# Two thirds of a modulation vector: summed over weight rows on GpSimd instead of TensorE

## The chip, the cores and the metric

The kernel runs on one core of one Trainium2 chip, in one launch. The metric is the device time of an execution in microseconds. TensorE is PE in the profile (PEld is its weight load), VectorE is DVE, ScalarE is ACT, GpSimd is POOL, and SyncE, which only issues transfers here, is SP.

## What is computed

One transformer block on 1024 tokens of width 1024, in fp32. A vector `c` gives six modulation vectors of 1024 (shift, scale and gate, for the mixer and for the feed-forward part); the mixer is a dilated attention with 8 heads beside a gated DeltaNet with 8 heads.

```python
c_act = jax.nn.silu(c)                        # c: (1, 1024)
mod = c_act @ w_ada[l] + b_ada[l]             # w_ada: 1024 x 6144
sh1, sc1, g1, sh2, sc2, g2 = [m[:, None, :] for m in jnp.split(mod, 6, axis=-1)]
h = _rmsnorm(x, norm_attn_g[l]) * (1.0 + sc1) + sh1
proj = h @ w_in[l]
q_a, k_a, v_a, q_d, k_d, v_d, z_d, b_d, a_d = jnp.split(proj, split_points, axis=-1)
y_attn = _dilated_attention(q_a, k_a, v_a, rel_bias)
y_delta = _gated_deltanet(q_d, k_d, v_d, z_d, b_d, a_d, ...)   # conv, chunked delta rule, gate z
x = x + g1 * (jnp.concatenate([y_attn, y_delta], axis=-1) @ w_out[l])
h = _rmsnorm(x, norm_ffn_g[l]) * (1.0 + sc2) + sh2
x = x + g2 * ((jax.nn.silu(h @ w_gate[l]) * (h @ w_up[l])) @ w_down[l])
return _rmsnorm(x, final_norm_g)
```

The change concerns `mod`. Only `sh1` and `sc1`, the first third, are needed before the projections. `g1`, `sh2`, `sc2` and `g2`, the last two thirds, are needed only after attention and DeltaNet.

## The kernel before

**Stages.** The first 16 column tiles of `mod` (a tile is 128 columns) are made at the start. Then come the projections, the DeltaNet in two groups of four heads (`delta(0)`, `delta(1)`), the attention in four pairs of heads (`attend`), the output projection, and from about 820 us on a feed-forward part, in which POOL has no instruction.

**Projections.** A weight slab of 128 x 512 is loaded on SP's queue into one of 3 buffers, copied by ACT to a rounded high part, and POOL subtracts to get the low part (`wsplit`, L209; subtraction L216; 5 buffers each for the two parts). TensorE multiplies high by high, high by low and low by high (`gemm`, L567, and `proj_t`, L590). The slabs of the delta projections of group 1 are named kd, qd and vd, those of the gates z0 and z1, those of the attention va (values) and a (keys and queries).

**Order.** Most of these projections are filler. `others()` (L1103) is a generator that yields after every few matmuls: z0; kd, qd and vd of group 1; z1; va; then the keys and queries of the four attention pairs. The DeltaNet and the attention are written in the order of their dependencies, and at named places (`turn`, `hold`, `until`, with amounts in microseconds from a table, `FILL`, and `LEVELS`) they take the next pieces from the generator. So TensorE's order is fixed when the program is built, and a matmul that waits holds up all behind it.

**The delta rule's chain.** For each group, a decay table goes out to `G_d` and comes back as `dt` tiles, masked by POOL (L692). `delta_inverse` inverts 32 x 32 triangles in 31 steps, each a multiplication (L862, `tm`) and an addition (L866, `tt`) on DVE. The result goes through DRAM and comes back as `tn`. Then four heads follow, staggered by `SKEW`: TensorE's `lv` (L894), `lw` (L923), `lx` (L931); DVE's transposes of `tn` into `U` (L899) and products (L905, L925); POOL clears `U` (L895) and part of `tc` (L896) first. A scan over chunks (`delta_scan`) follows. In attention, POOL and ACT share the scaling of the exponentials `X` (POOL L1263, ACT L1261), and POOL makes `KL` (L1227).

**The modulation before.** `modulation()` (L1081) has 64 steps: 8 groups `i` of four column tiles, times 8 blocks `k` of 128 rows. A step loads a 128 x 512 slab `wm` of `w_ada` (L1091, 256 KB) and issues `rows4` (L196): four matmuls, the slab as moving operand, and as weights a window of 32 columns of `cc`, the activated `c` laid out by blocks. The sums of a group gather in one PSUM bank. After eight steps DVE transposes them (`mt`, L203) and adds `b_ada` (L207). `mixed()` (L1123) wraps `others()`: whenever 1.9 us (`MODS`) of filler have been issued, and no head of the delta rule is being written (`quiet`), it issues the next step. What is left goes out ahead of the attention (`run(mods)`, L1193). The slabs share their three buffers (tag `tc`) with the `tc` tiles of the heads.

Of the kernel before, what the change touches and what calls it, by code (L numbers as in the profile page):

```python
# [18 lines left out]
P = 128  # L19
# [8 lines left out]
TCB = 3  # L28
MODS = 1.9
EARLY = 1  # L30
# [39 lines left out]
def build(tc, I, out):  # L70
# [47 lines left out]


    pd, sd = pool("pd")  # L120
    wp, swp = pool("wp", side="right")
# [23 lines left out]
    def ybank(name):  # L145
        return psb(name, "y", 1)
# [62 lines left out]
    def wsplit(src, n, name, eng=None, hurry=True):  # L209
        raw = wp.tile([P, slot], F32, name=f"wr_{name}", tag="wr", bufs=3)  # L210
        hi = wp.tile([P, slot], F32R, name=f"wh_{name}", tag="wh", bufs=5)
        lo = wp.tile([P, slot], F32R, name=f"wl_{name}", tag="wl", bufs=5)
        with urgent() if hurry else ExitStack():
            nc.sync.dma_start(raw[:, :n], src)
            nc.scalar.copy(hi[:, :n], raw[:, :n])
            (eng or nc.gpsimd).tensor_tensor(  # L216
                out=lo[:, :n], in0=raw[:, :n], in1=hi[:, :n].bitcast(F32), op=ALU.subtract
            )
        return hi, lo


# [621 lines left out]
    def delta_inverse(g, st):  # L843
# [92 lines left out]
        for step in range(3 * SKEW + 8):  # L936
            if step % SKEW == 0 and step // SKEW < 4:
                heads.append(head(step // SKEW))
            with hold(*LEVELS[g]) if step == 0 else ExitStack():
                quiet[0] = True  # L940
                for h in heads:
                    next(h, None)
        quiet[0] = False

# [135 lines left out]

    def modulation():  # L1081
        pm = ybank("mods")
        for i in range(8):
            t0 = 16 + 4 * i
            ps = pm[:, P * (i % 4) : P * (i % 4 + 1)]
            if i % 4 == 0:
                nc.vector.memset(pm, 0.0)
            for k in range(KT):
                w = pd.tile([P, HALF], F32, name=f"wm_{i}_{k}", tag="tc", bufs=TCB)
                with urgent():  # L1090
                    nc.sync.dma_start(w, I["wada"][k * P : (k + 1) * P, t0 * P : t0 * P + HALF])  # L1091
                rows4(ps, cc[:, k : k + 32], w, 4, k == KT - 1)
                yield
            t = pv.tile([P, 256], F32, name=f"mt{i}", tag="zt", bufs=2)
            by_columns(ps, mod[:, t0 : t0 + 4], 4, bada[:, t0 : t0 + 4], shape=t)
        nc.vector.scalar_tensor_tensor(
            out=G2, in0=mod[:, 32:40], scalar=1.0, in1=gff, op0=ALU.add, op1=ALU.mult
        )

    done = set()  # L1100
    mods = modulation()
# [90 lines left out]
    until(lambda: EARLY - 1 in done)  # L1192
    run(mods)  # L1193

# [149 lines left out]
    attend(range(EARLY))  # L1344
    run(fill[0])
    sh_.close()
    py, sy = pool("py", side="right")
# [18 lines left out]
    for k in range(EARLY):  # L1366
        y_load(k, _.ya[k])
    run(fill[0])

    ps = abank("g2t")  # L1370
# [4 lines left out]

    sa.close()
    syd.close()
    pf, sf = pool("pf")
# [503 lines left out]
```

## Time and profile before

| | |
|---|---|
| time, median of 3 executions | 1454.71 us (1454.52 to 1459.43) |
| the profiled execution's own time | 1459.26 us |
| its span, first to last instruction | 1457.5 us |
| mean granted TensorE clock | 0.975 of full speed |
| PE busy | 1381.9 us, 95% of the span |
| DVE, ACT, POOL busy | 872.7, 668.8, 284.5 us |
| POOL instructions | 267 |
| modulation's matmul records (L196) | 512, from 117.2 to 399.8 us, 8 a step |
| modulation's loads | 64 of 256 KB, 3.6 us from issue to landing |

A row of the profile's timelines gives the start, the duration, the engine, the line, the operation, output <- inputs, and, in brackets, the idle time of the engine just before it and what ended it. `x8` at the end of a row means that eight instructions that touch are shown as one. A row of groups gives, after `|`, the busy time in us and the mean of one instruction in ns, then the idle time before them.

### The profile page before, as it was taken

How to read it: one execution, taken by the hardware profiler on the slowest of the kernel's cores; microseconds unless marked ns; L12 is line 12 of the kernel's file. 1: busy time of each engine (PE TensorE's matmuls, PEld its weight loads, DVE VectorE, ACT ScalarE, POOL GpSimd, SP SyncE). 2: the span in 40 equal slices, each digit the busy share in tenths (PEclk: the TensorE clock that was granted, in tenths of full speed). 3: DMA queues.
4: the chain of work that ended last, by engine and by line, in shares of the span. 5: the costliest groups of instructions: out<-in, count | busy, mean ns of one | idle time of the engine just before them, and what ended most of it. 6: DMA issues, size and time to landing. Idle time of an engine off the chain costs nothing.

```text
span 1457.5 us, 24558 instructions
## 1 busy us (share of the span) xinstructions
PE 1381.9 (95%) x8984; PEld 1121.6 (77%) x8984; DVE 872.7 (60%) x1676; ACT 668.8 (46%) x1279; POOL 284.5 (20%) x267
## 2 busy tenths in 40 slices
PE   7998989998999989999999889999999999999997
PEld 4777857787888768778877668888888888888886
DVE  3686762665746151466426985767666676565477
ACT  3487513348233363566337733333333333444446
POOL 1343412243323333344244000000000000000000
PEclk9998999998999989999999989999999999999999
DMA  8736464465531626643275443545454465866566
GB/s 306 251 106 175 134 192 142 146 197 168 157 107 56 179 78 181 169 121 95 92 226 168 136 151 117 192 137 175 148 167 156 155 207 182 277 211 202 198 218 238
DMA packets 171345, 244.64 MB, mean 168 GB/s; under 512 B 33014, under 2 KB 76327, under 8 KB 171224
## 3 DMA queue, kind: packets, MB, share of 16 engines
q1 hardware_dynamic: 171224, 243.07, 53.0%
q8 instruction: 71, 1.16, 0.3%
q14 instruction: 50, 0.41, 0.1%
HBM read 180.25 MB, written 67.48 MB: 170 GB/s over the span
## 4 chain that ended last, share of the span: by engine, by line
PE 63%; DVE 6%; DMA 4%; ACT 3%; issue 2%; POOL 1%; SPq 0%; ACTq 0%; DVEq 0%; POOLq 0%
PE wga L1513 8%; PE wua L1513 8%; PE X L1699 6%; PE g_a L567 5%; PE wuc L1513 4%; PE wgc L1513 4%; PE Z L1699 4%; PE wo L567 4%; PE g_va L590 3%; PE y L1293 3%; PE tr L1276 2%; PE Y L1699 2%; PE wub L1513 2%; PE wgb L1513 2%; PE S L1252 1%
## 5 line engine op out<-in xcount | busy, mean ns | idle before, releaser
L1503 DVE TENSOR_TENSOR wl_db<-wr_db,wh_db 128x512 fp32r<-128x512 f32 x77 | 53.2, 691 | 75.6 <-ACT wh_db L1502 75.5
L1502 ACT CAST wh_db<-wr_db 128x512 fp32r<-128x512 f32 x77 | 47.9, 622 | 97.8 <-PE X L1699 41.3
L1699 PE MATMUL X<-wl_db,wh_da 128*128 128x512 f32 x176 | 68.5, 389 | 0.0
L1699 PE MATMUL X<-wh_db,wl_da 128*128 128x512 f32 x176 | 68.5, 389 | 0.0
L1699 PE MATMUL X<-wh_db,wh_da 128*128 128x512 f32 x176 | 68.5, 389 | 0.0
L1263 POOL TENSOR_SCALAR X<-X,sc 128x128 f32<-128x128 f32 (+7 forms) x64 | 47.6, 747 | 70.6 <-DVE sc L1262 56.2
L1261 ACT ACTIVATE X<-X,sc 128x128 f32<-128x128 f32 (+7 forms) x64 | 49.6, 776 | 22.4 <-DVE sc L1256 17.2
L1256 DVE CUSTOM_DVE_ANT_0 X<-S,ng 128x512 f32<-128x512 f32 (+3 forms) x64 | 36.8, 586 | 35.0 <-PE S L1253 26.3
L567 PE MATMUL wo<-yh,wh_wo 128*128 128x512 f32 x128 | 52.2, 409 | 3.7 <-ACT yh L1359 2.1
L1503 DVE TENSOR_TENSOR wl_da<-wr_da,wh_da 128x512 fp32r<-128x512 f32 x77 | 52.7, 686 | 1.2 <-ACT wh_da L1502 1.2
L567 PE MATMUL g_a<-hh,wh_a 128*128 128x512 f32 x128 | 51.4, 401 | 0.0
L567 PE MATMUL g_a<-hl,wh_a 128*128 128x512 f32 x128 | 51.1, 399 | 0.0
L567 PE MATMUL g_a<-hh,wl_a 128*128 128x512 f32 x128 | 51.0, 398 | 0.0
L567 PE MATMUL wo<-yl,wh_wo 128*128 128x512 f32 x128 | 51.0, 398 | 0.0
L567 PE MATMUL wo<-yh,wl_wo 128*128 128x512 f32 x128 | 50.5, 396 | 0.0
L1502 ACT CAST wh_da<-wr_da 128x512 fp32r<-128x512 f32 x77 | 47.4, 616 | 5.9 <-PE wua L1513 5.8
L1222 DVE SCALAR_TENSOR_TENSOR QS<-raw,QS 64x1024 fp32r<-64x1024 f32 x8 | 12.6, 1571 | 61.4 <-ACT QS L1221 61.4
L1502 ACT CAST wh_wg_s<-wg_s 128x512 fp32r<-128x512 f32 x33 | 20.5, 622 | 58.1 <-PE wuc L1513 22.6
L1293 PE MATMUL y<-et,va 128*64 128x128 f32 x576 | 46.7, 289 | 0.0
L1276 PE MATMUL tr<-ident,X 128*128 128x128 f32 x288 | 45.0, 282 | 1.6 <-ACT et L1281 1.2
L1502 ACT CAST wh_wg<-wr_wg 128x512 fp32r<-128x512 f32 x33 | 20.4, 622 | 51.4 <-issue 20.0
L1293 PEld LDWEIGHTS y<-et,va 128*64 128x64 f32 x576 | 35.0, 142 | 10.4 <-issue 8.8
(530 smaller groups left out, 4391.4 us busy)
## 6 DMA issues: line engine op xcount, KB each, us to landing
wr_da<-ao_d SPq DMA_DIRECT2D x77, 256.0 KB, 3.1
wm<-in_wada SPq DMA_DIRECT2D x64, 256.0 KB, 3.6
wr_wg<-in_wg SPq DMA_DIRECT2D x48, 256.0 KB, 2.9
wr_wu<-in_wu SPq DMA_DIRECT2D x48, 256.0 KB, 2.7
ao_d<-a SPq DMA_DIRECT2D x44, 256.0 KB, 2.2
wr_wd<-in_wdn SPq DMA_DIRECT2D x44, 256.0 KB, 3.0
wr_db<-wt_d SPq DMA_DIRECT2D x44, 256.0 KB, 2.6
ao_d<-as SPq DMA_DIRECT2D x33, 256.0 KB, 2.0
```

Of the source, the lines that this page charges most:

```text
L567: last[0] = nc.tensor.matmul(ps, a[:, w0], b[k0 + k4][:, cs], start=(i == 0), stop=(i == n - 1))
L590: last[0] = nc.tensor.matmul(ps[:, :n], a[k][:, ts_], b[:, w0], start=(i == 0), stop=(i == 23))
L1252: nc.tensor.matmul(ps[:, 0 : c1 - c0], QS[:, qs], KS[:, c0:c1], start=True, stop=False)
L1256: nc.vector.tensor_tensor_reduce(out=X[:, c0:c1], in0=ps[:, 0 : c1 - c0], in1=ng[:, u + c0 : u + c1], scale=1.0, scalar=(3e38 if m is None ...
L1261: nc.scalar.activation(X[:, 0:nk], X[:, 0:nk], AF.Exp, scale=-1.0, bias=m, accum_out=sc[:, 2:3])
L1263: nc.gpsimd.tensor_scalar(out=X[:, 0:nk], in0=X[:, 0:nk], scalar1=sc[:, 3:4], scalar2=0.0, op0=ALU.mult, op1=ALU.add)
L1276: nc.tensor.transpose(ps[:, (kb - c0) * P : (kb - c0 + 1) * P], X[:, kb * P : kb * P + P], ident)
L1293: nc.tensor.matmul(yps[64 * e : 64 * e + 64, yc], va[:, kb, 64 * e : 64 * e + 64], ets[e][:, kb, :], start=(kb == 0), stop=(kb == qb),)
L1502: nc.scalar.copy(hi, src)
L1503: (eng or nc.vector).tensor_tensor(out=lo, in0=src, in1=hi.bitcast(F32), op=ALU.subtract)
L1513: nc.tensor.matmul(ps, a[:, w0], b, start=(first and k == 0 and n_ == 0), stop=(k == 3 and n_ == 2), skip_group_check=True,)
L1699: nc.tensor.matmul(bank[b], a[:, ts_], w, start=(first and f == 0 and n_ == 0), stop=(f == NF - 1 and n_ == 2), skip_group_check=True,)
```

## The change

The 64 steps leave TensorE. A step is now tied to a weight slab: `wsplit`, after issuing its own load and subtraction, calls `mod_steps(steps[0], ...)`, which issues, for each step, the load of the slab `wm` two steps ahead, on SP behind the weight slab's load, and two instructions on GpSimd behind the subtraction: `wm` times the block's column of `c` (a scalar per partition), and for `k` > 0 an addition into an accumulator `wa` (at `k` = 0 the product is written there directly). There is one step with each slab until the values of attention, two with each slab of the keys and queries, and one with each of the first slabs of the output projection. The slabs have a pool of their own, `pm`: three buffers `wm` and four `wa`. When a group of column tiles is finished, five steps later `mod_columns` sums its accumulator over the partitions: four matmuls with 128 x 128 of the accumulator as weights and a column of ones, and an addition of `b_ada` on DVE. The last group's sums come just before `g2` is needed.

```diff
@@ wsplit
-            nc.sync.dma_start(raw[:, :n], src)
+            ld = nc.sync.dma_start(raw[:, :n], src)
             nc.scalar.copy(hi[:, :n], raw[:, :n])
-            (eng or nc.gpsimd).tensor_tensor(
+            sp = (eng or nc.gpsimd).tensor_tensor(
                 out=lo[:, :n], in0=raw[:, :n], in1=hi[:, :n].bitcast(F32), op=ALU.subtract
             )
+        if steps[0]:
+            mod_steps(steps[0], ld, sp)
         return hi, lo
+
+    steps = [0]
@@ modulation() removed, in its place:
+    MU = [(t0, k) for t0 in range(16, 48, 4) for k in range(KT)]
+    wms2, accs = {}, {}
+    at = [0]
...
+    def mod_load2(u):
+        if u < len(MU):
+            t0, k = MU[u]
+            wms2[u] = pm.tile([P, HALF], F32, name=f"wm_{t0}_{k}", tag="wm", bufs=3)
+            nc.sync.dma_start(wms2[u], I["wada"][k * P : (k + 1) * P, t0 * P : t0 * P + HALF])
+
+    def mod_steps(n, ld, sp):
+        for _n in range(n):
+            u = at[0]
+            if u == len(MU):
+                return
+            at[0] += 1
+            t0, k = MU[u]
+            with tc.issue_after(ld.ins):
+                if u == 0:
+                    mod_load2(0)
+                    mod_load2(1)
+                mod_load2(u + 2)
+            w = wms2.pop(u)
+            if k == 0:
+                accs[t0] = pm.tile([P, HALF], F32, name=f"wa_{t0}", tag="wa", bufs=4)
+            o = accs[t0] if k == 0 else w
+            with tc.issue_after(sp.ins):
+                nc.gpsimd.tensor_scalar(
+                    out=o, in0=w, scalar1=cc[:, k : k + 1], scalar2=0.0, op0=ALU.mult, op1=ALU.add
+                )
+                if k > 0:
+                    nc.gpsimd.tensor_tensor(out=accs[t0], in0=accs[t0], in1=w, op=ALU.add)
+            if k == 5 and t0 > 16:
+                mod_columns(t0 - 4)
+
+    def mod_columns(t0):
+        with tc.issue_after(last[0].ins):
+            ps = abank(f"mods{t0}")
+            for j in range(4):
+                nc.tensor.matmul(ps[:, j : j + 1], accs[t0][:, j * P : (j + 1) * P], ones[:, 0:1], start=True, stop=True)
+        nc.vector.tensor_tensor(out=mod[:, t0 : t0 + 4], in0=ps[:, 0:4], in1=bada[:, t0 : t0 + 4], op=ALU.add)
...
@@ others()
+        steps[0] = 1
         yield from proj_t(I["wz0"], 256, "z0", z_evac(0))
...
         done.add("va")
+        steps[0] = 2
         for hp in range(4):
...
-    def mixed():
-        t = 0.0
-        for c in others():
-            yield c
-            t += c
-            if t > MODS and not quiet[0]:
-                t = 0.0
-                next(mods, None)
-    quiet = [False]
-    fill[0] = mixed()
+    fill[0] = others()
@@ 
-    run(mods)
@@ after the first attention pair
+    steps[0] = 1
@@ after the last filler of attention
+    mod_columns(44)
```

The amounts in `FILL` and `LEVELS` are the same. A pool is opened and closed for `pm`, and the buffer that the program sets aside for dynamic transfers is given a size of 256, which leaves SBUF for it.

More of the change, by code (lines that the diff above doesn't have):

```diff
@@ L28 @@
 TCB = 3
-MODS = 1.9
 EARLY = 1
@@ L117, in small @@
         return t
+    pm, sm = pool("pm")
     pd, sd = pool("pd")
@@ L939, in delta_inverse @@
             with hold(*LEVELS[g]) if step == 0 else ExitStack():
-                quiet[0] = True
                 for h in heads:
                     next(h, None)
-        quiet[0] = False
     def delta_scan(g, st):
@@ L1078, in va_end @@
         return g
[L1081 to L1098, printed above, removed]
+    MU = [(t0, k) for t0 in range(16, 48, 4) for k in range(KT)]
@@ new lines, in build @@
+    wms2, accs = {}, {}
+    at = [0]
+    pmods = [None]
+    def mod_load2(u):
[27 more added lines that the diff above has]
+                mod_columns(t0 - 4)
@@ new lines, in mod_columns @@
+    def mod_columns(t0):
[4 more added lines that the diff above has]
+        nc.vector.tensor_tensor(out=mod[:, t0 : t0 + 4], in0=ps[:, 0:4], in1=bada[:, t0 : t0 + 4], op=ALU.add)
+        if t0 == 36:
+            nc.vector.scalar_tensor_tensor(
+                out=G2, in0=mod[:, 32:40], scalar=1.0, in1=gff, op0=ALU.add, op1=ALU.mult
+            )
@@ L1100, in build @@
     done = set()
-    mods = modulation()
     def others():
@@ L1368, in build @@
     run(fill[0])
+    assert at[0] == len(MU)
+    mod_columns(44)
     ps = abank("g2t")
@@ L1376, in build @@
     sa.close()
+    sm.close()
+    steps[0] = 0
     syd.close()
@@ L1870 @@
     from concourse.bass_utils import run_bass_kernel_spmd as _run
-    nc = _bacc.Bacc("TRN2", target_bir_lowering=False, num_devices=1)
+    nc = _bacc.Bacc("TRN2", target_bir_lowering=False, num_devices=1, dynamic_dma_scratch_size=256)
     arrays, aps = {}, {}
```

## The prediction

> **What bounds the kernel now.** I began with the page's busy shares, then cut the stretch in which the modulation runs into slices of 40 us, and read the timelines of three engines where two of them meet.
>
> ```profile
> PE 1381.9 (95%) x8984; PEld 1121.6 (77%) x8984; DVE 872.7 (60%) x1676; ACT 668.8 (46%) x1279; POOL 284.5 (20%) x267
> ```
>
> TensorE is busy for 95% of the span and GpSimd for 20%, so a change that takes work from the first to the second looks free. Two of the slices (columns: window, its length, busy time and instructions of PE, weight load, DVE, ACT, POOL, then granted clock, DMA share and GB/s) show that this isn't one regime.
>
> ```profile
> 160.00:200.00 40.00, 35.65 (x244) 26.30 (x243) 35.83 (x74) 8.88 (x17) 13.65 (x13) 0.91 0.54 162
> 200.00:240.00 40.00, 39.96 (x258) 26.94 (x258) 8.21 (x13) 11.07 (x24) 8.59 (x9) 1.00 0.79 230
> ```
>
> At 200 to 240 PE is full and DVE nearly empty: matrix work binds. At 160 to 200 DVE is the full one, with the inverse of the delta rule's first group (L862 and L866, 31 dependent steps). Which of the two arrives later at the next step that needs both, the heads at L894, is shown by the timelines of PE and of DVE before the first head.
>
> ```profile
> 238.39 0.39 PE L567 MATMUL g_vd<-hl,wh_vd 128*128 128x512 f32 x1
> 238.61 0.39 PE L567 MATMUL g_vd<-hh,wl_vd 128*128 128x512 f32 x1
> 238.93 0.43 PE L196 MATMUL mods<-wm,cc 128*32 128x128 f32 x8
> 239.29 0.50 PE L567 MATMUL g_vd<-hh,wh_vd 128*128 128x512 f32 x1
> 239.62 0.39 PE L567 MATMUL g_vd<-hl,wh_vd 128*128 128x512 f32 x1
> 239.86 0.39 PE L567 MATMUL g_vd<-hh,wl_vd 128*128 128x512 f32 x1
> ...
> 240.88 1.20 PE L894 MATMUL lv<-tn,dt 32*32 32x32 f32 x64
> ```
> ```profile
> 211.93 0.88 DVE L899 STREAM_TRANSPOSE U<-tn 32x256 f32<-32x256 f32 x2
> ...
> 214.08 0.44 DVE L899 STREAM_TRANSPOSE U<-tn 32x256 f32<-32x256 f32 x1
> 234.07 0.32 DVE L203 STREAM_TRANSPOSE mt<-mods 128x128 f32<-128x128 f32 x1 [19.54 <-PE mods L196]
> ```
>
> The inverse's result is in SBUF by 211.93, for DVE transposes it there, and is ready at 214.5; PE comes to the head only at 240.88. So the chain has about 26 us of slack at the first group, and PE sets the time. At the second group it is otherwise:
>
> ```profile
> 405.31 0.19 DVE L866 TENSOR_TENSOR tt<-tt,tm 128x31 f32<-128x31 f32 x1
> 413.37 1.78 DVE L899 STREAM_TRANSPOSE U<-tn 32x256 f32<-32x256 f32 x4 [7.86 <-DMA tn<-tn_d]
> 420.76 1.75 DVE L905 TENSOR_TENSOR cs<-lv,nbp 32x256 f32<-32x256 f32 x4 [5.61 <-PE lv L894]
> ```
>
> The transposes end at 415.15 and the head's first result comes 5.61 us later. The slack is about 5 us: less PE work is hardly felt there, and a later DVE is.
>
> **Removed from PE.** A step's eight matmul records stand between 512-column matmuls. Those follow each other in 0.22 to 0.24 us; across the step it is 0.68 (238.61 to 239.29), then 0.33. One step therefore takes 0.45 + 0.10 = 0.55 us. The records of the modulation by window, in the same columns without ACT and POOL, are
>
> ```profile
> 120.00:160.00 40.00, 3.81 (x56) 1.29 (x56) 0.00 (x0) 0.83 0.59 152
> 160.00:200.00 40.00, 5.15 (x88) 1.82 (x88) 0.61 (x2) 0.91 0.54 162
> 200.00:240.00 40.00, 6.39 (x120) 2.36 (x120) 1.12 (x3) 1.00 0.79 230
> ```
>
> 264 records at 8 a step are 33 of the 64 steps, 18.2 us before the first head. Two stalls of the modulation go as well:
>
> ```profile
> 136.17 0.63 PE L196 MATMUL mods<-wm,cc 128*32 128x128 f32 x8 [3.18 <-DMA wm<-in_wada]
> 191.43 0.65 PE L196 MATMUL mods<-wm,cc 128*32 128x128 f32 x8 [3.89 <-DVE mt L203]
> ```
>
> 7.1 us, so PE alone could be 25 us earlier at the first head; with the 31 later steps (17 us) the whole kernel has some 42 us to win.
>
> **Added to GpSimd.** Each step is one 128x512 multiplication by a scalar and, for seven of eight, one 128x512 addition. Rows of those shapes on POOL:
>
> ```profile
> L1263 POOL TENSOR_SCALAR X<-X,sc 128x512 f32<-128x512 f32 x8 | 5.5, 693 | 12.9 <-DVE sc L1262 8.0 <-PE S L1253 4.1 <-PE tr L1276 0.8
> L216 POOL TENSOR_TENSOR wl_vd<-wr_vd,wh_vd 128x512 fp32r<-128x512 f32 x4 | 5.1, 1284 | 23.1 <-ACT wh_vd L215 23.1
> ```
>
> 64 x 0.693 + 56 x 1.284 = 116 us, 1.98 us for a full step. POOL goes to about 400 us, far from full, so its throughput isn't the matter. What matters is who waits while it is busy. The first cost is DVE: in the inverse, an instruction of this size passes in 0.41 us (183.78), except beside POOL's subtractions.
>
> ```profile
> 182.37 1.37 DVE L862 TENSOR_TENSOR tm<-nt,tt 128x240 f32<-128x240 f32 x1
> 183.78 0.41 DVE L866 TENSOR_TENSOR tt<-tt,tm 128x240 f32<-128x240 f32 x1
> ...
> 185.58 1.45 DVE L866 TENSOR_TENSOR tt<-tt,tm 128x252 f32<-128x252 f32 x1
> ```
> ```profile
> 169.12 4.69 POOL L216 TENSOR_TENSOR wl_kd<-wr_kd,wh_kd 128x512 fp32r<-128x512 f32 x3
> 173.76 0.74 POOL L612 TENSOR_TENSOR zt<-zt,ngh 128x256 f32<-128x256 f32 x1
> 174.58 1.29 POOL L216 TENSOR_TENSOR wl_qd<-wr_qd,wh_qd 128x512 fp32r<-128x512 f32 x1
> 182.10 1.38 POOL L216 TENSOR_TENSOR wl_qd<-wr_qd,wh_qd 128x512 fp32r<-128x512 f32 x1 [6.23 <-ACT wh_qd L215]
> 185.46 1.29 POOL L216 TENSOR_TENSOR wl_qd<-wr_qd,wh_qd 128x512 fp32r<-128x512 f32 x1 [1.99 <-ACT wh_qd L215]
> ```
>
> The DVE instruction at 182.37 lies under POOL's at 182.10, the one at 185.58 under 185.46; together they lose 2.0 us to 2.67 us of POOL, 0.75 us for each. I take 0.75 for all of a step. The Trainium skill ("SBUF — State Buffer", section "Who interferes with whom") says that a DVE instruction with two SBUF inputs and a GpSimd instruction that reads SBUF exclude each other for a whole instruction. By that rule a step would cost the chain up to 1.98 us rather than 1.5; the row has 0.75 of it, and the sum goes by the row.
>
> Six of the slabs' subtractions lie in this inverse, and each now has a step behind it; with one from a later slab I count seven. 7 x 1.98 x 0.75 = 10.4 us on the first inverse (7 if only the additions block, 14 if all does). Ahead of it, three of the modulation's loads now wait on the SP queue for GpSimd's additions to free their buffers, and in the changed order the decay table's store and load (G_d, dt) stand behind them there, which the chain needs before the inverse: at most three steps of 1.98 us, so 0 to 6; I take 3. The chain is ready for the head at 214.5 + 10 + 3 = 228 instead of 214.5. PE comes there at 240.9 - 25 = 216. So the chain takes over as the bound, and the first head is 13 us earlier, not 25. If its first matmul needs the inverse alone and not the transposes, the gain is 3 to 5 us larger: I take 15 (8 to 25).
>
> **From the first heads to the second inverse.** About half of the 31 later steps go from PE here (9 us), but the order in which the changed program issues puts 6 to 12 us more projection work ahead of this group's preparation. I take 0, from -5 to +9.
>
> **Second inverse and heads.** Five steps behind the wva slabs: 5 x 1.98 x 0.75 = 7.4 us; the slack of 5 takes up most, so 2.5 (0 to 8). Then the heads clear U on POOL, in the midst of their chain:
>
> ```profile
> 424.55 0.96 POOL L895 MEMSET U<- 128x1024 f32 x1 [20.79 <-PE lw L923]
> 426.92 0.30 POOL L896 MEMSET tc<- 32x256 f32 x1 [1.41 <-PE lx L931]
> 430.15 0.96 POOL L895 MEMSET U<- 128x1024 f32 x1 [2.93 <-PE lw L923]
> ```
>
> They come 5.6 us apart. In the changed order the second one stands behind five slab subtractions (5 x 1.28) and their steps, one of which waits for PE to free its buffer just after the head's first matmul: I count a good 6 us (0 to 8). Before the third stand two steps, 4 us, and before the fourth three, 5.9 us, about what there is room for. In the scan, 1 us (0 to 3).
>
> **Attention and the sums over partitions.** 3 us of the projections are done earlier by the new order: +3 (0 to 5). In the first attention the scaling of X on POOL (L1263) waits behind steps of 2 us; four or five fall there, and PE's other projections hide some: 4 us (0 to 8), and 1 later (0 to 3). The 32 one-column matmuls are new; the nearest row is
>
> ```profile
> L1451 PE MATMUL ssq<-onesr,acc x16: 166/250/271, 771.3 to 801.8; 128*128 128x1 f32 x16
> ```
>
> two records a matmul: at 0.25 us a record 16 us if all were exposed and none overlapped. They overlap their neighbours and half lie where the chain binds: 1.5 us (0 to 12; no gain is possible in added work). The vanished transposes, additions and memsets of DVE were between other waits: 0.
>
> **Sum.** +15 + 0 - 2.5 - 6 - 1 + 3 - 4 - 1 - 1.5 = 2 us gained. The profiled execution took 1459.26 us with a span of 1457.5; it goes to about 1457. It was 4.5 us over the median of the three, 1454.71, so the median goes to **1452.7**. The ends of the terms together are a gain of 39 and a loss of 39; they won't all fall on one side, and about half of that, 20, is the likeliest case's own range: 1433 to 1473.
>
> **Rivals.** (1) *TensorE stays the bound everywhere*: DVE slips into the gaps between POOL's instructions, the memsets find POOL free, and most of the 42 us comes through, less the columns: 20 to 40 us, 1415 to 1435. For it: PE 95% busy, 26 us of slack at the first heads. Against: 5 us of slack at the second. (2) *GpSimd becomes a link of the chain.* Its place is the second group's heads and the first attention: its queue runs in order, so the three memsets and the eight rounds of X each wait for a whole step with the weight slab it stands behind. Price: 3 x 5 for the heads, 12 for attention, 8 for the inverse, against 13 gained at the first heads: a loss of 22, 1477; between 10 and 30 by how many steps fall just ahead. It decides once POOL reaches the second head's memset later than 5.6 us after the first. For it: five slabs and steps are queued there. Against: POOL idles 20.79 us before 424.55, so it may have run ahead. (3) *The matmuls removed were hidden*, and every stall that goes comes back as the next wait: nothing within 2 us, 1455. Against it, the full PE at 200 to 240.
>
> **Chances.** The forecast 0.43, of which within 0.5% (7.3 us, about what a measurement of this kernel can tell from no change) 0.28, faster 0.09, slower 0.06; rival 1 0.26, all faster; rival 2 0.27, nearly all slower (0.26, and 0.01 within); rival 3 0.04, within. So faster 0.35, same 0.33, slower 0.32. The range reaches half into each of rivals 1 and 2, 1424 to 1475.
>
> **What would show it.** Right: no L196 in the changed profile after the start; POOL near 400 us; the first L894 near 226 with DVE's idle of 19.54 ahead of it gone; the inverse of the first group about 10 us longer than its 30; the second group's memsets late against the first by over 5.6 us; TensorE's idle time larger than before ahead of both heads. The scaling would be wrong if POOL's 128x512 instructions take over 2 us each, the split if PE is full up to the heads (rival 1), and the whole if most of the loss or gain lies in the feed-forward part, in which the change issues nothing.

## The result, and the profile after

The change made the kernel slower: a median of 1492.80 us (1490.78 to 1497.06, four executions) against 1454.62 us, a ratio of 1.025 [1.0217, 1.0283]. The prediction was 1452.7 us, 1424 to 1475. The profiled execution took 1497.06 us, with a span of 1495.3 us against 1457.5. Ratios, here and below, leave out executions at a lowered clock, which the medians beside them hold; with two of the experiments (x1 and x10) that makes a difference.

The page of the changed kernel, busy shares:

```profile
PE 1369.9 (92%) x8536; PEld 1128.3 (75%) x8536; DVE 893.5 (60%) x1666; ACT 667.6 (45%) x1279; POOL 412.0 (28%) x387
```

TensorE has 448 matmul records fewer and is busy for 12 us less, and the span is 37.8 us longer. GpSimd's new work, in the groups by shape, is what was forecast, a little dearer (127.6 us together against 116):

```profile
L1116 POOL TENSOR_TENSOR wa<-wa,wm 128x512 f32<-128x512 f32 x56 | 76.3, 1363 | 2.9
L1112 POOL TENSOR_SCALAR wm<-wm,cc 128x512 f32<-128x512 f32 x56 | 44.0, 790 | 13.3 <-DMA wm<-in_wada 13.2
L1112 POOL TENSOR_SCALAR wa<-wm,cc 128x512 f32<-128x512 f32 x8 | 7.3, 912 | 0.0
```

The two slices of 40 us, in the columns of the prediction:

```profile
160.00:200.00 40.00, 37.70 (x262) 33.47 (x260) 32.60 (x37) 11.71 (x19) 28.11 (x25) 0.96 0.41 116
200.00:240.00 40.00, 27.91 (x114) 22.61 (x113) 27.93 (x53) 10.56 (x23) 16.81 (x15) 0.83 0.54 157
```

In the first, DVE is nearly as busy as before with half the instructions (37 against 74). In the second, where PE was full, it is now idle for 12 us. The timeline of PE shows where:

```profile
144.47 1.12 PE L718 MATMUL trq_0False<-ident,qd 128*128 128x128 f32 x4 [15.87 <-ACT qd L540]
...
214.71 0.39 PE L571 MATMUL g_qd<-hh,wl_qd 128*128 128x512 f32 x1
227.19 0.80 PE L571 MATMUL g_qd<-hh,wh_qd 128*128 128x512 f32 x1 [12.09 <-ACT sp_qd L1069]
...
246.79 1.20 PE L898 MATMUL lv<-tn,dt 32*32 32x32 f32 x64
```

The first head's matmul, forecast near 226, comes at 246.79, against 240.88 before. The timelines of DVE and of ACT show why TensorE stood still ahead of it:

```profile
222.57 0.19 DVE L870 TENSOR_TENSOR tt<-tt,tm 128x31 f32<-128x31 f32 x1
226.64 5.13 DVE L536 SCALAR_TENSOR_TENSOR cv<-xp_k,cw,cv 128x1023 f32<-128x1023 f32 x3 [3.88 <-ACT cv L534]
231.69 1.78 DVE L903 STREAM_TRANSPOSE U<-tn 32x256 f32<-32x256 f32 x4
```
```profile
225.46 1.15 ACT L534 ACTIVATE cv<-xp_k,cw 128x1024 f32<-128x1024 f32 x1 [17.43 <-DMA tn_d<-tt]
226.51 0.63 ACT L1069 COPY sp_qd<-g_qd 128x256 f32<-128x256 f32 x2
```

The convolution of group 1 (`cv`) uses one of the two buffers of the inverse (both have the tag `dt`). ACT waits for that buffer until the inverse is done and stored, 17.43 us, and behind it in ACT's queue stands the copy of `g_qd` that frees the PSUM bank for TensorE's next projection. So a longer inverse stops TensorE's filler too. The 26 us of slack that I read off the timelines of before was not room for the inverse: work that fills TensorE up to the head hangs on the same inverse.

Landmarks from the timelines of the profiled executions, in us (an inverse counts from its first multiplication to the end of its last addition, a head by its product `cs`, an attention pair by its first score matmul, and `ssq` are the sums of squares before the feed-forward part):

| | before | after | later by |
|---|---|---|---|
| inverse 0 starts | 170.3 | 182.2 | 11.9 |
| inverse 0 ends | 200.2 | 222.8 | 22.6 |
| first head | 241.6 | 247.5 | 5.9 |
| inverse 1 starts | 377.5 | 391.9 | 14.4 |
| inverse 1 ends | 405.5 | 428.1 | 22.6 |
| last head of group 1 | 434.4 | 454.3 | 19.9 |
| attention starts | 508.3 | 531.9 | 23.6 |
| second pair | 599.3 | 628.0 | 28.7 |
| last pair | 669.2 | 705.7 | 36.5 |
| `ssq` | 771.3 | 806.5 | 35.2 |
| span | 1457.5 | 1495.3 | 37.8 |

By `ssq` 35.2 of the 37.8 us are lost, and they are gathered bit by bit.

### The profile page after: what moved, and what is told of

It reads as the page before. It is cut to its first block, busy times and chain, and to the rows that moved or that the text cites. A ratio compares the mean times of both kernels' runs of the same rounds, so it can differ in the third digit from the quotient of the medians.

```text
span 1495.3 us, 23742 instructions
## 1 busy us (share of the span) xinstructions
PE 1369.9 (92%) x8536; PEld 1128.3 (75%) x8536; DVE 893.5 (60%) x1666; ACT 667.6 (45%) x1279; POOL 412.0 (28%) x387
## 4 chain that ended last, share of the span: by engine, by line
PE 50%; DVE 4%; DMA 4%; POOL 3%; issue 2%; ACT 2%; SPq 0%; ACTq 0%; DVEq 0%; POOLq 0%
PE wga L1539 8%; PE wua L1539 8%; PE X L1725 6%; PE wuc L1539 4%; PE wgc L1539 4%; PE Z L1725 4%; PE wo L571 3%; PE y L1314 2%; PE wgb L1539 2%; PE Y L1725 2%; PE tr L1297 2%; PE wub L1539 2%; POOL wa L1116 1%; PE g_a L571 1%; DMA raw<-qk_d 1%
## 5 line engine op out<-in xcount | busy, mean ns | idle before, releaser
L1116 POOL TENSOR_TENSOR wa<-wa,wm 128x512 f32<-128x512 f32 x56 | 76.3, 1363 | 2.9
L1282 ACT ACTIVATE X<-X,sc 128x128 f32<-128x128 f32 (+7 forms) x64 | 49.5, 774 | 19.9 <-DVE sc L1277 15.7
L216 POOL TENSOR_TENSOR wl_wo<-wr_wo,wh_wo 128x512 fp32r<-128x512 f32 x24 | 32.9, 1374 | 59.3 <-ACT wh_wo L215 52.6
L1112 POOL TENSOR_SCALAR wm<-wm,cc 128x512 f32<-128x512 f32 x56 | 44.0, 790 | 13.3 <-DMA wm<-in_wada 13.2
L1273 PE MATMUL S<-KS,QS 128*128 128x512 f32 (+3 forms) x96 | 36.9, 393 | 11.6 <-DVE sc L1277 5.9
```

What stands on the lines that cost most here:

```text
L1112: nc.gpsimd.tensor_scalar(out=o, in0=w, scalar1=cc[:, k : k + 1], scalar2=0.0, op0=ALU.mult, op1=ALU.add)
L1116: nc.gpsimd.tensor_tensor(out=accs[t0], in0=accs[t0], in1=w, op=ALU.add)
L1273: nc.tensor.matmul(ps[:, 0 : c1 - c0], QS[:, qs], KS[:, c0:c1], start=True, stop=False)
L1282: nc.scalar.activation(X[:, 0:nk], X[:, 0:nk], AF.Exp, scale=-1.0, bias=m, accum_out=sc[:, 2:3])
```

## Experiments

Ratios are to the kernel before, run beside each, with 95% intervals.

**Which part costs: loads, arithmetic, or the missing matmuls.** First the change without its GpSimd arithmetic; the loads and the sums over partitions stay. The diffs here and below show the lines that matter.

```diff
-                nc.gpsimd.tensor_scalar(out=o, in0=w, scalar1=cc[:, k : k + 1], ...)
-                if k > 0:
-                    nc.gpsimd.tensor_tensor(out=accs[t0], in0=accs[t0], in1=w, op=ALU.add)
+            if k == 0:
+                accs[t0] = w
```

> The changed kernel without the 120 GpSimd instructions: the loads and the sums over partitions stay, and each accumulator holds its first slab instead of the weighted sum of eight, so seven eighths of the last two thirds of the modulation are left out. ScalarE's order is that of the changed kernel (the exponential of the decay table, L819, ahead of a convolution's silu; the first convolution of group 1, L534, ahead of an eviction of g_qd). Theory A, GpSimd's arithmetic is what costs (it holds the loads on SP, shuts VectorE out in the inverse, and so makes ScalarE and then TensorE wait): 1425 to 1440 us, with TensorE's stalls of 15.87 and 12.09 us before the first head gone or under 4 each. Theory B, the new order of instructions on ScalarE costs by itself: the two stalls stay over 8 us each and the time stays over 1470. Theory C, the loads beside each weight slab cost (SP's queue, transfers): 1460 or more with the stalls elsewhere.

Measured: 1461.91 us, ratio 0.9993 [0.9955, 1.0032]. The loss is gone, so it is in the arithmetic. Yet nothing is won: its ten executions spread from 1450.6 us (granted clock 0.973) to 1478.1 (0.951). In the profiled one, at 1450.6, the first head comes 16.7 us earlier than before (224.9), `ssq` 10.7 earlier, the end 8.6. TensorE's timeline shows what took the place of the matmuls:

```profile
137.02 1.11 PE L718 MATMUL trq_0False<-ident,qd 128*128 128x128 f32 x4 [9.28 <-ACT qd L540]
...
205.09 0.55 PE L571 MATMUL g_qd<-hh,wh_qd 128*128 128x512 f32 x1 [4.77 <-ACT sp_qd L1069]
```

Then the converse twice: the changed kernel with the arithmetic on one slab that is loaded once, and the kernel before, its matmuls and loads as they were, with the same 120 GpSimd instructions beside it to no use.

```diff
@@ x2: the changed kernel
-                mod_load2(u + 2)
-            w = wms2.pop(u)
+            w = wk[0]                      # one slab, loaded once
@@ x3: the kernel before, in wsplit, behind the subtraction
+        if steps[0]:
+            extra(steps[0], sp)            # the same multiplication and addition, on one slab
```

> The changed kernel with all 120 GpSimd instructions, but each works on one slab loaded once: 63 of the 64 loads are left out, and nothing on SP waits for GpSimd's additions. Theory A1, the loads queued on SP behind the additions are the larger part (the decay table 7 us late, ScalarE 9.9 us, TensorE 15.9 us): 1455 to 1470. Theory A2, the exclusion of VectorE in the inverse and the queue on GpSimd are the larger part: 1475 to 1490, with the first inverse still about 40 us long.

> The kernel before, whose modulation stays on TensorE, with the same 120 GpSimd instructions behind the same weight slabs, on one slab loaded once, to no use. ScalarE's order is that of the kernel before. Theory A: the first inverse grows from 30 to about 40 us and is hidden in the 26 us of slack, the second from 28 to 36 with 5 us of slack, and the memsets come 3 us late: 1462 to 1478. Theory B (only the new order costs): 1454 to 1460, no change.

Measured: 1498.19 us, 1.028 [1.0221, 1.0339], and 1503.69 us, 1.0311 [1.0277, 1.0345]. The loads' place on SP is not needed for the loss, nor is the changed order of TensorE. 125 us of GpSimd work beside a kernel in which nobody waits for its result cost 45 us.

**GpSimd's queue, or its reading.** Two ways are open: others wait behind GpSimd's instructions in its queue, or GpSimd's reads of SBUF hold VectorE up. Memsets of the same duration keep the queue and read nothing.

```diff
@@ x8: x2 with
-                nc.gpsimd.tensor_scalar(out=o, in0=w, ...)
+                nc.gpsimd.memset(accs[t0] if k == 0 else wk[0][:, 0:711], 0.0)
-                    nc.gpsimd.tensor_tensor(out=accs[t0], in0=accs[t0], in1=o, op=ALU.add)
+                    nc.gpsimd.memset(wk[0][:, 0:1402], 0.0)
@@ x12: x2 with
-                    nc.gpsimd.tensor_tensor(out=accs[t0], in0=accs[t0], in1=o, op=ALU.add)
+                    nc.gpsimd.memset(wz[0], 0.0)          # 128 x 1402
```

> The changed kernel with each of the 120 GpSimd instructions replaced by a memset of about the same length (711 elements a partition for a multiplication of 0.69 us, 1402 for an addition of 1.28, 512 for the first of a group), and without the 64 loads: GpSimd is as long busy and its queue as long as in the run without loads (1498 us), but its new instructions read nothing from SBUF. The modulation's last two thirds are left out. Theory A2a, the exclusion of VectorE (GpSimd reads while VectorE wants two inputs) is the larger part of the cost: 1455 to 1472, and the first inverse is 30 us long as in the run without arithmetic. Theory A2b, the in-order queue of GpSimd (weight parts, masks, memsets and X behind the steps) is the larger part: 1482 to 1500.

> The run without loads, with only the 56 additions replaced by memsets of their length (1402 elements): the 64 multiplications still read SBUF, one input each. The modulation's last two thirds are left out. If any GpSimd instruction that reads SBUF excludes VectorE for its time, the cost follows the time spent reading: 64 x 0.69 = 44 of 116 us, 38% of the 37 us between the runs with memsets alone (1461) and without loads (1498): about 1475 (1468 to 1482). If an instruction with one input excludes nothing: 1458 to 1464. If what costs is not the time of reading but that every slab has some reading behind it: 1490 or more.

Measured: 1460.85 us, 1.0038 [1.0005, 1.0071], for memsets alone: 114 us in GpSimd's queue cost 0.4%. With the multiplications back, reading one input each, 1451.18 us, 0.9967 [0.9942, 0.9993]: no loss at all, a miss of what I expected. Inside this run's first inverse, though, each kind of GpSimd instruction can be read beside VectorE's (timelines of DVE and of POOL):

```profile
180.73 0.32 DVE L870 TENSOR_TENSOR tt<-tt,tm 128x156 f32<-128x156 f32 x1
181.09 0.34 DVE L866 TENSOR_TENSOR tm<-nt,tt 128x175 f32<-128x175 f32 x1
181.47 0.79 DVE L870 TENSOR_TENSOR tt<-tt,tm 128x175 f32<-128x175 f32 x1
...
184.27 1.36 DVE L866 TENSOR_TENSOR tm<-nt,tt 128x220 f32<-128x220 f32 x1
```
```profile
180.13 1.27 POOL L1117 MEMSET wz<- 128x1402 f32 x1
181.38 0.69 POOL L1113 TENSOR_SCALAR wm<-wk,cc 128x512 f32<-128x512 f32 x1
...
183.98 1.40 POOL L216 TENSOR_TENSOR wl_qd<-wr_qd,wh_qd 128x512 fp32r<-128x512 f32 x1
```

Beside the memset an instruction of VectorE passes in 0.32 to 0.34 us; beside the one-input multiplication the same size takes 0.79, and beside the two-input subtraction 1.36. So reading is what blocks, with one input as with two, and it blocks for about what is left of the GpSimd instruction.

These kernels interleave TensorE's filler in different ways, by hundreds of lines, so their totals compare orders as well as reads. The last set leaves the order alone: the kernel before with memsets, with one-input instructions, and with additions whose multiplications are memsets. In the traces the last two keep the order of x3 on PE, ACT, DVE and SP (one pair of matmul records apart); the one with memsets differs by two lines on PE, by the places of eight instructions on ACT and of a few transfers on SP, and by none on DVE.

```diff
@@ x17: x3 with memsets for both
+                nc.gpsimd.memset(wk[0][:, 0:512], 0.0)
+                    nc.gpsimd.memset(wk[0][:, 0:640], 0.0)
@@ x18: x3 with a second one-input instruction for the addition
+                    nc.gpsimd.tensor_scalar(out=accs[t0], in0=o, scalar1=cc[:, k : k + 1], ...)
@@ x19: x3 with a memset for the multiplication
+                nc.gpsimd.memset(o, 0.0)
```

> The kernel before with 64 memsets of 512 and 56 of 640 elements on GpSimd behind the weight slabs (64 x 0.52 + 56 x 0.63 = 69 us of its queue, no reading), in the instruction order of the run before-plus-arithmetic (1504 us). If GpSimd's occupied queue costs: in proportion to 116 us for 44, 1475 to 1490. If reading costs: 1453 to 1463, as the kernel before.

> The kernel before with 120 one-input multiplications of 128x512 on GpSimd (64 x 0.69 + 56 x 0.69 = 83 us, all of it reading one input), in the same order as the run before-plus-arithmetic. If the time of reading costs, whatever the number of inputs: 83 of 116 us of a loss of 44, 1480 to 1492. If only the additions with two inputs cost: 1455 to 1466.

> The kernel before with the 56 two-input additions and memsets in place of the multiplications, in the same order as the run before-plus-arithmetic. If the time of reading costs: 72 of 116 us of a loss of 44, 1478 to 1488. If only instructions with two inputs cost: all of the loss, 1490 to 1504.

| | added on GpSimd | of it reading | us | ratio |
|---|---|---|---|---|
| x17, memsets | 69.0 us | 0 | 1458.53 | 1.0026 [1.0005, 1.0048] |
| x18, one input | 93.1 us | 93.1 | 1485.97 | 1.0214 [1.0176, 1.0251] |
| x19, additions | 108.3 us | 75.6 | 1487.84 | 1.0227 [1.0196, 1.0259] |
| x3, both | 125.4 us | 125.4 | 1503.69 | 1.0311 [1.0277, 1.0345] |

Over x17 that is 27, 29 and 42 us lost for 93, 76 and 125 us of reading: 0.29, 0.39 and 0.33 us for each. The intervals, some 0.4% wide to each side of such a difference, don't tell one input from two. x17 holds the queue for less time than the other three; x8, which holds it for 114 us at the same 0.4%, speaks for the queue being cheap there too, though in another order. The first inverse in these four, cut to its own stretch (the windows of x17, x18, x19 and x3, in the columns above):

```profile
167.00:196.90 29.90, 26.00 (x161) 17.49 (x160) 27.87 (x64) 4.70 (x11) 14.19 (x18) 0.94 0.59 177
...
237.10:371.80 134.70, 124.21 (x1319) 103.92 (x1312) 79.64 (x168) 67.93 (x140) 57.90 (x61) 0.96 0.54 161
```
```profile
172.80:206.80 34.00, 26.01 (x157) 17.33 (x156) 31.97 (x64) 4.70 (x11) 16.14 (x18) 0.85 0.48 154
```
```profile
171.40:207.20 35.80, 29.93 (x178) 20.11 (x178) 33.76 (x64) 5.33 (x12) 18.90 (x20) 0.90 0.50 159
```
```profile
175.30:212.20 36.90, 26.05 (x156) 17.34 (x155) 34.82 (x64) 4.67 (x11) 18.85 (x18) 0.86 0.44 141
254.30:400.50 146.20, 132.21 (x1340) 110.45 (x1333) 79.94 (x169) 68.25 (x141) 65.06 (x61) 0.92 0.50 148
```

The same 64 instructions of VectorE take 27.87 us beside memsets and 34.82 beside the arithmetic, and the inverse is 7.0 us longer, all of it VectorE's own busy time. From the first head to the second inverse (the second row of x17 and of x3) another 11.5 us are lost, and there VectorE's busy time is the same, 79.64 and 79.94. Part of it is waits on GpSimd's queue at the end of the stretch. The timelines of DVE in x17 and in x3, and of POOL in x3:

```profile
370.43 1.23 DVE L873 TENSOR_TENSOR nt<-nt,bpr 128x1024 f32<-128x1024 f32 x1 [3.85 <-DMA nt<-lt_d]
371.81 0.19 DVE L884 TENSOR_TENSOR tm<-nt,tt 128x31 f32<-128x31 f32 x1 [0.16 <-POOL tt L879]
```
```profile
396.43 1.23 DVE L879 TENSOR_TENSOR nt<-nt,bpr 128x1024 f32<-128x1024 f32 x1 [5.50 <-POOL wx L247]
400.49 0.19 DVE L890 TENSOR_TENSOR tm<-nt,tt 128x31 f32<-128x31 f32 x1 [2.84 <-POOL tt L885]
```
```profile
396.83 1.97 POOL L217 TENSOR_TENSOR wl_va<-wr_va,wh_va 128x512 fp32r<-128x512 f32 x1
...
400.31 0.15 POOL L885 MEMSET tt<- 128x32 f32 x1
```

GpSimd clears `tt` late, behind a subtraction that VectorE's own instruction stretched from 1.28 to 1.97 us: 2.7 us more there and 1.7 more at `nt`. In the rest TensorE takes 8.0 us longer for 1340 matmul records instead of 1319, at a granted clock of 0.92 instead of 0.96; what the clock has to do with waits is shown further down.

**Other places and another engine.** The first five steps left out and made up later, which frees the decay table's store from them; then no step at all before the keys and queries of attention, with three to a slab there.

```diff
@@ x4
+            if skip[0]:
+                skip[0] -= 1               # 5 at the start
+                continue
@@ x9
-        steps[0] = 1                       # ahead of wz0
-        steps[0] = 2
+        steps[0] = 3                       # ahead of the keys and queries
@@ both: after the first attention pair
-    steps[0] = 1
+    steps[0] = 2
```

> The changed kernel without the first five steps: they start once the decay table is out, and are made up at the end by two steps a slab in the output projection. Theory: G_d goes out about 6 us earlier, ScalarE's wait of 9.93 us for it and TensorE's of 15.87 shrink, and the first inverse starts at 172 to 176 instead of 182; of these 8 us at most half reach the end, since each later stage keeps its own cost: 1486 to 1492. If the late start is what all later delays come from: 1475 to 1482.

> The changed kernel with no step before the attention's keys and queries, then three a slab, and two a slab in the output projection: none falls into the first inverse, few into the second. Theory A: up to the second heads it runs like the kernel without arithmetic (first head at 225, second inverse from 362), 36 us ahead of the changed kernel; then all 64 steps lie in the second heads, the scan and the first attention and cost 15 to 30 there: 1462 to 1480. Rival: the cost is the same wherever the steps lie (1490 to 1500).

Measured: 1515.77 us, 1.0418 [1.0387, 1.0448], and 1506.20 us, 1.0338 [1.0303, 1.0373]: both worse than the change. In x4 the table's store comes at 116.11, as before (116.06), instead of 122.96, and the first inverse starts at 176.3 instead of 182.2; the gain is gone by the last head of group 1 (455.1 against 454.3). In x9 the second inverse starts at 365.2, 12.3 us earlier than before, so the removed matmuls do pay as long as no arithmetic stands beside; but from the first head of group 1 to attention it takes 120.9 us (406.4 to 527.3) instead of 87.5. A cost moves along with the steps; how much of it is GpSimd's reading is taken up below.

VectorE instead of GpSimd, with one fused instruction a step, where the change has them, and late:

```diff
@@ x7
-                    nc.gpsimd.tensor_scalar(...); nc.gpsimd.tensor_tensor(...)
+                    nc.vector.scalar_tensor_tensor(
+                        out=accs[t0], in0=w, scalar=cc[:, k : k + 1], in1=accs[t0], op0=ALU.mult, op1=ALU.add)
@@ x13: x7, with x9's places and x11's hold
```

> The changed kernel with each step as one instruction on VectorE (product and sum in one, 128x512, 0.69 to 0.75 us by the row of L1503) in place of two on GpSimd: 64 x 0.72 = 46 us on VectorE, no new GpSimd work. Theory A2a: the first inverse is 7 x 0.72 = 5 us longer than without steps (36), the second 4 us; 1452 to 1470. Theory A2b: GpSimd's queue is free again, the same 1452 to 1470 or below. If the cost lies in neither but in work beside the chains on any engine: 1480 or more.

> The whole modulation computed, each step as one instruction on VectorE, none before the attention's keys and queries, three a slab then and two a slab in the output projection, with the exponential behind the silu. Up to the second heads it should run as the run without arithmetic (first head near 220, second inverse near 358); from there 64 x 0.72 = 46 us of VectorE, of which the part in the second heads and the scan (some 20 steps, 14 us) stands in the chain and the part beside TensorE's projections (VectorE 10% busy at 560 to 600 before) is hidden: 1442 to 1458, at best 1% below the kernel before. Rival: VectorE's part stays on the path in attention as well: 1465 to 1480.

Measured: 1476.58 us, 1.0141 [1.0115, 1.0168], and 1454.22 us, 0.9995 [0.9968, 1.0022]. The work costs VectorE 0.84 us a step (46.8 us for 56) where GpSimd takes 2.15, and a good half of the loss is left. Late and with the waits put right the version draws level with the kernel before; it is the best found of those that compute all of the modulation, and no gain.

**Waits and a slower clock.** These totals hold two kinds of loss. The pages of the profiled executions give the time that TensorE is busy, and the rest of the span it is idle. The clock records of the traces stand at full or at half clock, and at nothing between. (In the last column, the half-clock stretch that outlasts the span is left out.)

| | span, us | TensorE busy | idle | at half clock |
|---|---|---|---|---|
| before | 1457.5 | 1381.9 | 75.6 | 68 |
| x17, memsets | 1459.5 | 1388.1 | 71.4 | 79 |
| x3, arithmetic | 1504.0 | 1399.5 | 104.5 | 116 |
| x1, the change without arithmetic | 1448.9 | 1358.0 | 90.9 | 75 |
| the change | 1495.3 | 1369.9 | 125.4 | 120 |
| x4 | 1514.2 | 1390.9 | 123.3 | 167 |
| x9 | 1507.1 | 1391.3 | 115.8 | 150 |
| x7 | 1475.4 | 1388.7 | 86.7 | 140 |

With the arithmetic TensorE is idle for 33 us more (x3 over x17) and 34 us more (the change over x1), and busy for 11 and 12 us more with as many matmuls. x4 and x9 are idle no longer than the change; they are slower than it by 21 us of busy time each. x7 is idle for less than x1, so all that it loses against x1 is busy time. For the stage from the first head of group 1 to attention, the window of the kernel before, and a window and a row of PE's timeline of x9:

```profile
420.80:508.30 87.50, 84.90 (x848) 73.50 (x841) 38.64 (x113) 29.66 (x75) 30.01 (x31) 1.00 0.35 103
```
```profile
417.00:458.00 41.00, 40.68 (x371) 31.96 (x371) 10.65 (x28) 7.44 (x19) 24.33 (x27) 0.50 0.35 102
```
```profile
417.32 0.23 PE L913 MATMUL lv<-cs,U 32*32 32x32 f32 x1 [2.26 <-DVE U L903]
```

In x9 TensorE runs 41 us of this stage at half clock, behind a wait of 2.26 us. All 12 half-clock stretches of the change, and 12 of the 13 of x3, begin during an idle stretch of TensorE of over 1.5 us or within 3.5 us of its end. So a wait often costs twice, once as idle time and once as slower matmuls. Why the half clock lasts 41 us in this place and 3.4 in others isn't shown. So x4, x9 and x7 don't tell how the price of a step depends on its place or its engine.

**The two waits of TensorE.** The convolution's buffer of its own, which takes away the wait of 17.43 us; and the exponential of `eb` held behind the activation of `qd`, which the changed order had put ahead of it:

```profile
139.70 1.28 ACT L819 ACT_TABLE_LOAD   x1 [9.93 <-DMA eb<-G_d]
...
143.37 1.06 ACT L540 ACTIVATE qd<-qd 128x1024 f32<-128x1024 f32 x1
```

```diff
@@ x5
-            name=f"cv{j}", tag="dt", bufs=2
+            name=f"cv{j}", tag="cv", bufs=1
@@ x10 (on x1) and x11 (on the change)
+            with tc.issue_after(silu[0].ins):
                 nc.scalar.activation(eb, eb, AF.Exp)
```

> The changed kernel, with the four convolutions of group 1 in a buffer of their own instead of the two that the inverse holds (and three accumulators instead of four). Theory A: the wait of ScalarE for the inverse's transfer (17.43 us) goes, and with it TensorE's 12.09 us at 227; the head then waits for the chain at about 234 instead of 247, and 8 to 12 us of it come through: 1480 to 1486. Rival: TensorE has as much to wait for elsewhere (the chain of the second group is as late): 1490 to 1494, no change.

> The run without arithmetic (seven eighths of the modulation's last two thirds left out), with the exponential of the decay rows (L819) held on ScalarE behind the convolution's silu, where the kernel before has it. Theory: TensorE's wait of 9.3 us for qd, 137 to 146 in the runs, goes, and the first inverse starts some 6 to 9 us earlier, at 161 to 164 instead of 170; of it 3 to 8 us reach the end: 1442 to 1456 where the run without arithmetic had 1450 to 1473. Rival: the chain of the second group, whose transfers it then waits for, takes it back: no change.

> The changed kernel with the same exponential held behind the silu, nothing left out. Theory: TensorE's 15.87 us at 144 shrink to under 6 and the first inverse starts at 172 to 176 instead of 182, but VectorE is shut out for as long as before: 1482 to 1490. Rival, the stall in front is the cause of the loss: 1465 to 1475. Rival, other instructions move with it and cost as much: 1490 to 1510.

Measured: x5 1509.77 us, 1.0349 [1.0293, 1.0405], worse than the change. Its ACT timeline shows the wait in another form:

```profile
207.68 1.16 ACT L534 ACTIVATE cv<-xp_k,cw 128x1024 f32<-128x1024 f32 x1 [4.31 <-DMA xp_k<-pj_d]
...
224.17 1.06 ACT L540 ACTIVATE cv<-cv 128x1024 f32<-128x1024 f32 x1 [13.76 <-DVE cv L536]
225.13 0.63 ACT L1069 COPY sp_qd<-g_qd 128x256 f32<-128x256 f32 x2
```

ACT starts the convolution early and then waits for VectorE's part of it, which VectorE does in the midst of the inverse (44.8 us long instead of 40.5); the PSUM copy stands behind that. TensorE is idle for 124.2 us, as in the change (125.4), and busy for 1379.3 instead of 1369.9 us; that is what makes x5 the slower one. x10 gave 1459.70 us, 0.9937 [0.9902, 0.9973], at best 1442.32; x11 1489.51 us, 1.0214 [1.0186, 1.0241]. In x11 the transposes of `qd` come 12 us earlier (132.5), the first inverse only 2 (180.1). So the order of ACT is worth at most some 0.6%: x10 stands 0.6% below x1, and x11 0.4% below the change, with intervals that overlap.

## Why the prediction was wrong

It failed at two steps, which overlap. The first is **"Added to GpSimd"**: it charged the exclusion of VectorE in the two inverses, 17.8 us, and at no other place.

- *In the inverses it was right.* Forecast +10.4 and +7.4 us; measured 40.5 against 29.9 and 36.2 against 28.0, so +10.6 and +8.2. That the first fits so closely is partly luck: 17 us more of GpSimd's reading lay in it, not 13.9, at 0.63 us for each and not 0.75. The timelines of DVE and of POOL of the changed kernel show the same lock as the two rows of before that gave the 0.75:

```profile
187.94 0.67 DVE L866 TENSOR_TENSOR tm<-nt,tt 128x112 f32<-128x112 f32 x1
188.64 1.25 DVE L870 TENSOR_TENSOR tt<-tt,tm 128x112 f32<-128x112 f32 x1
189.93 1.26 DVE L866 TENSOR_TENSOR tm<-nt,tt 128x135 f32<-128x135 f32 x1
191.23 1.28 DVE L870 TENSOR_TENSOR tt<-tt,tm 128x135 f32<-128x135 f32 x1
```
```profile
187.12 1.37 POOL L1112 TENSOR_SCALAR wm<-wm,cc 128x512 f32<-128x512 f32 x2
188.45 1.31 POOL L1116 TENSOR_TENSOR wa<-wa,wm 128x512 f32<-128x512 f32 x1
189.72 1.31 POOL L216 TENSOR_TENSOR wl_qd<-wr_qd,wh_qd 128x512 fp32r<-128x512 f32 x1
190.99 1.35 POOL L1116 TENSOR_TENSOR wa<-wa,wm 128x512 f32<-128x512 f32 x1
```

VectorE gets one instruction through for each of GpSimd's. The rule cited from the Trainium skill ("SBUF — State Buffer", "Who interferes with whom") names GpSimd instructions that read and leaves out those that only write; x12's rows and x17 agree with both halves. I had used it for the inverses alone, where my two rows came from.

- *Outside the inverses* I had this exclusion at nothing. From x17 to x3 the span grows by 44.5 us, and the two inverses by 7.0 and 2.0. The other stages of x3 lose 8.3 us ahead of the first inverse, 1.9 up to the first head, 11.5 to the second inverse, 6.2 from its end to attention and 9.6 from there to `ssq`; 2.0 us are won behind that.

- *Ahead of the first inverse* I took 3 us, from 0 to 6, for loads of the modulation that wait on the SP queue for GpSimd's additions. It was 11.9, and those loads aren't needed for it. The decay table's store leaves at 122.96 instead of 116.06:

```profile
122.58 0.33 SPq L1092 DMA_DIRECT2D wm<-in_wada  x1
122.96 0.48 SPq L670 DMA_DIRECT2D G_d<-GT  x1
```

But it is as late in x2, at 122.66, where these loads are left out, and in x3, at 121.84, where they have the places of before. There it stands behind the weight slabs' own loads, each of which waits until GpSimd's subtraction has freed a slab buffer (the timelines of SP and of POOL in x3):

```profile
106.02 15.77 SPq L215 DMA_DIRECT2D wr_kd<-in_wd  x4
121.84 0.48 SPq L694 DMA_DIRECT2D G_d<-GT  x1
```
```profile
112.06 1.66 POOL L243 TENSOR_SCALAR wy<-wk,cc 128x512 f32<-128x512 f32 x1
113.81 2.13 POOL L247 TENSOR_TENSOR wx<-wx,wy 128x512 f32<-128x512 f32 x1
```

The subtraction stands behind a step, and the step takes longer here than the 0.69 and 1.28 us that I had read, beside VectorE's convolutions. Beside memsets the store leaves at 116.16 (x17) and 115.99 (x8). 5.9 us of the delay go when the first five steps are left out (x4), and x3 starts this inverse 8.3 us later than x17 (175.3 against 167.0). The store isn't all: x8, in its own order, starts the inverse at 175.7 in spite of its early store.

- *First head to second inverse*: forecast 0, from -5 to +9; a loss of 8.5. *Heads of group 1*: forecast a loss of 6 for the late clearing of U; after the inverse they took 2.7 us less than before. U was cleared 5.8 and 6.9 us apart, little over the 5.6 of before. *Scan and projections*: +2 forecast, 3.7 lost. *First attention pair*: 4 forecast, 5.1 lost. *Later pairs*: 1 forecast, 7.8 lost; here two steps go with each slab. *The one-column sums*: 1.5 forecast, nothing that stands out.

The second failed step is **"Removed from PE"** with its conclusion "PE alone could be 25 us earlier at the first head", and the slack of 26 us on which the trade rested. Forecast: first head 15 us earlier; measured: 5.9 later, which is 20.9 of the 40 us between forecast and result, part of it by way of the late and longer inverse of the first step. Without the arithmetic (x1) the head is 16.7 us earlier, not 25, since waits for ACT of 9.3 and 4.8 us take the place of the matmuls, and of the 42 us to be won over the whole kernel 8.6 are left at the end of the profiled execution and none in the median. Rival 3 ("the matmuls removed were hidden") describes x1. With the arithmetic the same two waits grew to 15.87 and 12.09 us: TensorE's arrival and the chain's were added up as if they were independent, while TensorE's filler hung on the inverse through ACT's queue.

Rival 2 had the right sign, and at 1477 a good half of the loss, but its mechanism, GpSimd's queue alone, is not the cause: 114 us of memsets in that queue cost 0.4%, and U, its place, was hardly late. The queue has a part where what stands in it reads: in x3 some 4 us ahead of the second inverse, and the slab loads that hold the table's store. Among the signs named beforehand, the longer inverse and PE's longer idle time ahead of both heads came true; the head at 226 did not, and U's gap passed its 5.6 us by far less than the 6 us forecast.

So the loss of 38 us is the price of GpSimd's reading: 42 us on the kernel before (x3 over x17), and in the change 42 or 37 us (x2, or the change itself, over x1, 1.0287 and 1.0257). In the profiled executions 11 to 12 us of it are matmuls at a lower clock, and the rest is TensorE's idle time. The gain from the shorter matmul work doesn't show in the medians.

Open: why x12, in its own order, lost nothing with 50 us of one-input reading, when x18 lost 27 us with 93; by which waits the reading outside the inverses reaches the end; and how long the half clock lasts behind a wait. VectorE's busy time grew by only 11.5 us from x17 to x3, while TensorE's idle time grew by 33, so most of the price is waits passed on; I followed only those at `nt` and `tt` and the table's store.

## What to carry to other kernels

An idle engine isn't free room: work for GpSimd that reads SBUF beside a VectorE with dependent two-input instructions can be priced by its reading time: here 0.3 to 0.4 us of the whole for each us in x18, x19 and x3, though nothing in x12. Slack between two engines can be spent only once it is known what else hangs on the later one: follow the queue of the engine between them (here ACT's, with a PSUM copy behind a wait for a buffer). A dummy that holds the queue for as long without reading (a memset), put into the unchanged kernel, tells queue from contention before anything is rebuilt. And where two totals are compared for their waits, TensorE's busy time and its granted clock belong beside them.

## What was not expected of the hardware

A GpSimd memset of 1.27 us beside VectorE's chain left its instructions at 0.32 to 0.34 us, while a one-input multiplication of 0.69 us held one for 0.79: with one input read as with two, VectorE's instruction waited; beside the memset it didn't. The block goes both ways: GpSimd's 128x512 subtraction, 1.28 us alone, took 1.97 us beside VectorE's 1024-column product. And behind a wait of TensorE of 2.26 us its clock was half for 41 us (x9).
